# Both layers' first two output blocks as a Strassen pair, with both output pairs' P1 and P2 in front, in a two-layer trunk kernel on one core

## The chip, the cores and the metric

The kernel runs on one core of a Trainium2 chip. The metric is the device time of one execution in microseconds (us). A core has a matrix engine (TensorE, PE in the profile; its weight loads are listed apart as PEld), a vector engine (VectorE, DVE), a scalar engine (ScalarE, ACT), a general engine (GpSimd, POOL) and a synchronising engine (SyncE, SP), each with an instruction stream of its own that it works off in order. Here SP issues the loads from device memory, and POOL most of the writes. TensorE adds up its results in PSUM; the kernel uses eight banks of 128 x 512 float32.

## The reference

Two layers of a streaming encoder over 512 tokens of width 2048. One input projection per layer, then a group of four gated-linear-attention (GLA) heads and a group of eight chunked-attention heads, then one output projection with a norm and the residual:

```python
def hybrid_layer(x, w_in, w_out, g_pre, g_post, w_alpha, b_alpha, g_gla, g_att, rel_bias):
    h = rmsnorm(x, g_pre)
    z = h @ w_in
    gq, gk, gv, gg, ga, aq, ak, av, ag = split_columns(z)
    ...
    o_gla = rmsnorm(o_gla, g_gla...) * jax.nn.silu(gg)
    o_att = rmsnorm(o_att, g_att...) * jax.nn.silu(ag)
    y = jnp.concatenate([o_gla, o_att], axis=-1) @ w_out
    return x + rmsnorm(y, g_post)
```

The GLA state runs over chunks of 64 tokens, `S_c = a_c * S_(c-1) + k_c^T v_c`, so the second half of the tokens needs the state at the end of the first.

## The kernel before

**Jobs.** All projections are cut into blocks of 512 output columns: fourteen of the input, then four of the output, W0 to W3 (`NB_IN` to `NB_IN + 3`). The unit of the stream of weights is a *job* (`class Job`, L174): 256 rows by 512 columns of weights (512 KB). SP loads it (`raw`, for a Strassen product also `H`), VectorE forms a sum or difference of two blocks where a product needs one (L240, L243), ScalarE writes the rounded high part `wh` (L251), VectorE the rest as low part `wl` (L257, three buffers in turn, L255). TensorE multiplies high by high, high by low and low by high, so that the result is near to float32. `prepare` and `ahead` (L285, L299) keep loads and parts a few jobs in front of TensorE.

**Two ways to multiply.** A block on its own (`std_gemm`, L360; matmuls L380) takes eight jobs of 24 matmuls. Two blocks together can be done as a Strassen pair (`class Pair`, L406; matmuls L504, or L491 with features on the partitions): seven products P1 to P7 over four chunks each, 28 jobs of 12 matmuls, where two single blocks take 16 jobs of 24. P1, P2 and P4 use the operands as they are (P4 with a combined weight); P5, P6, P3 and P7 use the sums S1 to S4 of quarters of the left operand. P1+P2 is token half 0 of the first block, P7, P3 and P4 close the other three. A pair has two pairs of PSUM banks, X and Y: P1 goes to X, P5 to Y, P6 to X, and so on (`target`, L414). `seeded` means that P2 goes on in the banks of P1, and that these are seeded again from a copy of P1 later (`open`, L435).

**Stages of a layer.** Three input pairs whose P1 and P2 stand in front of everything (`HEAD`), two pairs for queries and keys, one for the GLA keys and queries, one for the GLA values (GV0, GV1; order P1, P5, P6 and P3 mixed, P7, P2, P4 by `PROD`, L145). Then the output projection: W0 for all tokens, W1 for token tiles 0 and 1, the pair W2 and W3 (`W23`, order P1, P2, P5, P6 and P3 mixed, P7, P4 by `PROD_END`, L152), W1 again for token tiles 2 and 3 with its weights read a second time.

**Around the output projection.** The GLA heads are worked in units of one head and one token half (`class Unit`, L1238; `gla_heads`, L1336), both halves of two heads in a row once their value block is there. `output_sums` (L804, through `make_sums`, L753) loads the finished heads from memory (`t<-fa`, `t<-fg`), forms S1 to S4 of the output pair on VectorE (L765), splits each into high and low (L113, L114) in slots g0 to g3, and writes them out (`oS<-g`, POOL); SP loads them again as left operands (`sa<-oS`, L230). `project` (L1426) takes a closed PSUM bank out: ScalarE squares it for the norm (L1433), VectorE multiplies it by the gain (L1436). The gain is loaded by `load_gain` (L1420) into a tile from `t2()` (L77), a pool of eight buffers used in turn, which the four parts of every chunk of the sums and the squares use too. `finish` (L1463) ends with `finish_token` (L1447): norm, residual, and the write of a token tile (128 tokens) to memory. Work beside the matmuls (heads, sums, finishing) stands in a list of tasks that is worked off at a rate per job; the order on each engine comes from a scheduler over the recorded program.

## Time and profile before

| | |
|---|---|
| time, median of 3 runs | 1603.68 us (1603.67 to 1607.72) |
| profiled execution | 1604.27 us |
| its span, first to last instruction | 1601.9 us |
| TensorE's mean granted clock | 0.998 |
| loaded from and written to memory | 393.01 MB, 72.11 MB |

A row of a group of instructions reads: line, engine, operation, what it writes and reads, shape, number | busy us, mean ns of one | idle time of the engine just before them and what ended most of it. Names are those of the program without their numbers, and a number behind "x" is a count. A matmul's mean is longer than the distance between two of them, since they overlap. In the windows each engine has its busy us with the number of instructions, and behind them the granted clock (1.00 is full), the share of the sixteen DMA engines and GB/s.

### The profile page before, as it was taken

The numbers are of one execution on the slowest core, as the hardware profiler recorded it, in microseconds if no ns is written. First come the engines' busy times: TensorE is split into PE (matmuls) and PEld (weight loads), VectorE is DVE, ScalarE is ACT, GpSimd is POOL, SyncE is SP. The second block draws the span as 40 slices with busy tenths as digits, with TensorE's granted clock in tenths as the row PEclk, the third lists the DMA queues.
The fourth block names the chain that finished last, engine by engine and source line by source line (L and its number), as shares of the span: only waits on it lengthen the run. The fifth ranks groups of instructions, "written<-read, shape, count | busy, mean of one in ns | idle before, by whom it ended". The sixth has DMA issues, their size and how long they took to land.

```text
span 1601.9 us, 24514 instructions
## 1 busy us (share of the span) xinstructions
PE 1588.1 (99%) x8818; PEld 1353.9 (85%) x8818; DVE 1258.1 (79%) x1580; ACT 924.1 (58%) x1534; POOL 189.1 (12%) x302
## 2 busy tenths in 40 slices
PE   9999999999999999999999999999999999999997
PEld 6787889999988887788887888899999888777886
DVE  6888887786877876778868989768778778866886
ACT  8565544456676544555685556445666765355543
POOL 1131000001101101310312100000000011013110
PEclk9999999999999999999999999999999999999999
DMA  9999966858868698799868899668588677979995
GB/s 373 358 337 347 337 220 247 306 188 288 296 216 282 219 345 302 274 376 335 346 241 333 305 345 334 228 228 306 187 312 281 223 263 248 352 241 351 367 330 214
DMA packets 150616, 467.82 MB, mean 292 GB/s; under 512 B 16492, under 2 KB 35956, under 8 KB 150496
## 3 DMA queue, kind: packets, MB, share of 16 engines
q1 hardware_dynamic: 127232, 385.79, 67.7%
q0 software_dynamic: 22688, 79.53, 13.0%
q8 instruction: 69, 1.13, 0.3%
q10 hardware_dynamic: 576, 0.95, 0.2%
q14 instruction: 51, 0.42, 0.1%
HBM read 393.01 MB, written 72.11 MB: 290 GB/s over the span
## 4 chain that ended last, share of the span: by engine, by line
PE 92%; issue 3%; DMA 2%; DVE 1%; POOL 1%; ACT 1%; SPq 0%; POOLq 0%; DVEq 0%
PE mm L504 49%; PE mm L491 20%; PE mm L380 11%; PE ax L1089 2%; PE ax L504 1%; PE ax L1072 1%; PE ax L1255 1%; PE ax L1289 1%; DMA raw<-in_w_dram 1%; DMA H<-in_w_dram 1%; PE ax L1051 1%; PE ax L1052 1%; PE ax L1050 1%; PE ax L687 0%; DVE wl L257 0%
## 5 line engine op out<-in xcount | busy, mean ns | idle before, releaser
L251 ACT CAST wh<-raw 128x1024 fp32r<-128x1024 f32 x256 | 269.3, 1053 | 234.0 <-PE mm L504 97.3
L257 DVE TENSOR_TENSOR wl<-raw,wh 128x1024 fp32r<-128x1024 f32 x256 | 312.5, 1221 | 114.9 <-PE mm L504 36.2
L251 ACT CAST wh<-H 128x1024 fp32r<-128x1024 f32 x239 | 251.1, 1053 | 211.7 <-PE mm L504 88.7
L257 DVE TENSOR_TENSOR wl<-H,wh 128x1024 fp32r<-128x1024 f32 (+1 forms) x241 | 292.9, 1217 | 91.1 <-PE mm L504 36.5
L504 PE MATMUL mm<-wh,sa 128*128 128x512 f32 x1088 | 345.2, 392 | 0.1
L504 PE MATMUL mm<-wh,g 128*128 128x512 f32 x832 | 258.1, 389 | 0.0
L504 PEld LDWEIGHTS mm<-wh,sa 128*128 128x128 f32 x1088 | 203.2, 188 | 43.3 <-issue 1.5
L491 PE MATMUL mm<-sa,wh 128*128 128x256 f32 x1280 | 235.9, 285 | 0.0
L504 PE MATMUL mm<-wh,a 128*128 128x512 f32 x704 | 228.8, 396 | 2.2 <-ACT a L113 0.9
L504 PE MATMUL mm<-wl,sa 128*128 128x512 f32 x544 | 212.6, 391 | 0.0
L240 DVE TENSOR_TENSOR H<-H,raw 128x1024 f32<-128x1024 f32 x160 | 194.3, 1220 | 17.5 <-DMA raw<-in_w_dram 9.4
L491 PEld LDWEIGHTS mm<-sa,wh 128*128 128x128 f32 x1280 | 199.4, 192 | 0.3
L504 PEld LDWEIGHTS mm<-wh,g 128*128 128x128 f32 x832 | 156.2, 188 | 32.3
L491 PE MATMUL mm<-sa,wl 128*128 128x256 f32 x640 | 181.0, 283 | 0.0
L504 PE MATMUL mm<-wl,g 128*128 128x512 f32 x416 | 162.3, 390 | 1.1 <-DVE wl L257 1.1
L504 PEld LDWEIGHTS mm<-wh,a 128*128 128x128 f32 x704 | 131.6, 188 | 35.4 <-issue 4.9
L504 PE MATMUL mm<-wl,a 128*128 128x512 f32 x352 | 137.9, 393 | 0.6 <-DVE wl L257 0.5
L491 PEld LDWEIGHTS mm<-sa,wl 128*128 128x128 f32 x640 | 122.3, 191 | 0.1
L504 PEld LDWEIGHTS mm<-wl,sa 128*128 128x128 f32 x544 | 102.2, 188 | 21.3 <-DVE wl L257 0.3
L552 POOL TENSOR_TENSOR sm<-sm,cst 128x4 f32<-128x4 f32 (+2 forms) x40 | 59.4, 1486 | 321.6 <-DVE sm L1449 128.0
L491 PE MATMUL mm<-a,wh 128*128 128x256 f32 x512 | 94.4, 285 | 0.0
L504 PEld LDWEIGHTS mm<-wl,g 128*128 128x128 f32 x416 | 78.1, 188 | 18.9 <-DVE wl L257 2.6
(208 smaller groups left out, 2272.0 us busy)
## 6 DMA issues: line engine op xcount, KB each, us to landing
raw<-in_w_dram SPq DMA_DIRECT2D x352, 512.0 KB, 5.5
sa<-S SPq DMA_DIRECT2D x128, 512.0 KB, 4.7
H<-in_w_dram SPq DMA_DIRECT2D x63, 512.0 KB, 5.6
S<-g POOLq DMA_DIRECT2D x32, 512.0 KB, 6.4
g<-S SPq DMA_DIRECT2D x32, 512.0 KB, 5.2
sa<-A SPq DMA_DIRECT2D x32, 512.0 KB, 6.1
oS<-g POOLq DMA_DIRECT2D x32, 512.0 KB, 5.8
sa<-oS SPq DMA_DIRECT2D x32, 512.0 KB, 5.0
```

Of the source, the lines that this page charges most:

```text
L240: nc.vector.tensor_tensor(out=h, in0=h, in1=r, op=ALU.add)
L251: last_cast[0] = nc.scalar.copy(self.wh, src).ins
L257: last_low[0] = nc.vector.tensor_tensor(out=self.wl[:, kk, :], in0=self.src[:, kk, :], in1=self.wh[:, kk, :].bitcast(F32), op=ALU.subtract ...
L380: mm = nc.tensor.matmul(pss[o], a[:, part, t], rhs[:, kk, :], start=(i == 0 and kk == 0 and m == 0), stop=(i == n - 1 and kk == 1 and m == 2),
L491: nc.tensor.matmul(dst, lhs[:, kk, f], a[:, part, tok], start=(fresh and kk == 0 and m == 0 and ft % 2 == 0), stop=(c == self.last and kk ...
L504: nc.tensor.matmul(out_ps[t], a[:, part, tok], rhs[:, kk, :], start=(fresh and kk == 0 and m == 0), stop=(c == self.last and kk == 1 and m ...
L552: return nc.gpsimd.tensor_tensor(out=out_r, in0=v, in1=mhalf[:, : v.shape[-1]], op=ALU.pow).ins
L1050: nc.tensor.matmul(ps[:, :n], self.qh[:, t], self.kh[:, :n], start=True, stop=False)
L1051: nc.tensor.matmul(ps[:, :n], self.qh[:, t], self.kl[:, :n], start=False, stop=False)
L1052: nc.tensor.matmul(ps[:, :n], self.ql[:, t], self.kh[:, :n], start=False, stop=True)
L1072: nc.tensor.transpose(ps[:, j * P : (j + 1) * P], self.prob[i][:, j * P : (j + 1) * P], ident)
L1089: nc.tensor.matmul(o, self.pt[i][:, j * P : (j + 1) * P], av[hd // 4, j // 2][:, j % 2, (hd % 4) * P : (hd % 4 + 1) * P], start=(j == 0), ...
```

## The change

W0 and W1 become a Strassen pair as W2 and W3 are, in both layers (`PAIRED`). The stream of the output projection is now: W23's P1, W01's P1, W23's P2, W01's P2 (four jobs each), then the rest of W01 (P5, P6 and P3, P7, P4), then the rest of W23, 56 jobs of 12 matmuls. `paired_out` drives it and takes the place of the two `std_gemm` calls, of `w_consume` and of the second reading of W1. The value pair becomes an early, seeded pair: P1, P2, then the rest. The GLA units are started by token half: as soon as token half 0 of a value block is there, its two heads' first halves run, and `ends` keeps their last states for the second halves. The output sums are staged in g6, g7, g14 and g15. In the last layer the last three jobs of P4 are done bank by bank (`by_bank`), so that token tile 2 is taken out while tile 3 is multiplied. The core of the diff:

```diff
+    W01 = (NB_IN, NB_IN + 1)
     W23 = (NB_IN + 2, NB_IN + 3)
+    OUT = (W01[0], W23[0])
+    PAIRED = (0, 1)
...
         for b0, b1 in PAIRS:
-            pr = {"early": False}
-            stream += [Job(l, k, c, b0, b1, pr) for k, c in PROD]
+            pr = {"early": b0 == GV0}
+            order = early_head(C_IN) + early_rest(C_IN) if pr["early"] else PROD
+            stream += [Job(l, k, c, b0, b1, pr) for k, c in order]
+        if l in PAIRED:
+            outs = [(W01, {"early": True}), (W23, {"early": True, "second": True})]
+            for k, i in (("P1", 1), ("P1", 0), ("P2", 1), ("P2", 0)):
+                stream += [Job(l, k, c, *outs[i][0], outs[i][1]) for c in C_END]
+            for bs, pr in outs:
+                stream += [Job(l, k, c, *bs, pr) for k, c in early_rest(C_END)]
+            continue
...
+        def by_bank(self, prods, evac):
+            jobs = [take(self.l, self.b0, k, c) for k, c in prods]
+            closing = None
+            for t in range(2):
+                for job, (k, c) in zip(jobs, prods):
+                    with tc.issue_after(closing) if closing else nullcontext():
+                        self.matmuls(job, k, c, only=t)
+                closing = self.closing
+                evac(t, self.acc[self.target[k]][t])
...
-        return make_sums(l, True, ("g0", "g1", "g2", "g3"), parts, chunks)
+        return make_sums(l, True, ("g6", "g7", "g14", "g15") if l in PAIRED else ("g0", "g1", "g2", "g3"), parts, chunks)
...
-                for half in range(2):
+                for half in range(1 if paired else 2):
...
+        og, issued = {}, {"outer": 0, "states": 0}
+        ends = slot("g3", [4, 256])
...
+                if p == 0:
+                    self.st[3] = ends[:, h, :]
+                self.prev = ends[:, h, :] if p else None
...
-            yield from output_sums(l, (2,3,))
+            while not paired and issued["states"] < 8:
+                yield
+            yield from output_sums(l, (2, 3))
+            if paired:
+                while len(og) < 8:
+                    yield
+                yield from output_sums(l, (0, 1))
...
-        GV = {1: ("g4", "g5"), 0: ("g0", "g1")}
+        GV = {(0, 0): "g2", (1, 0): "g4", (1, 1): "g5", (0, 1): "g0"}
...
-            if h and t:
-                heads = gla_heads(j, [gv[j, p] for p in range(2)])
-                tasks.append(heads if j else beside(heads, early_sums(), 3))
+            if t:
+                heads = gla_heads([(2 * j, h), (2 * j + 1, h)])
+                tasks.append(beside(heads, early_sums(), 3) if (j, h) == (0, 1) else heads)
...
         def finish(pair, xs):
-            p4 = next(i for i, z in enumerate(stream) if z.l == l and z.b0 == W23[0] and z.kind == "P4")
-            while done["low"] < p4 + 4:
+            at, n = (("P4", 2) if last else ("P7", 2)) if paired else ("P4", 4)
+            first = next(i for i, z in enumerate(stream) if z.l == l and z.b0 == W23[0] and z.kind == at)
+            while done["low"] < first + n:
                 yield
...
+        def paired_out():
+            gains, held = {}, {}
+
+            def consume(n):
+                def f(j, h, t, src, comb):
+                    until(lambda: issued["states"] == 8)
+                    project(2 * h + t, n + j, settled(src, comb), gains[n + j])
+                    if (n + j, h, t) == (3, 0, 1):
+                        for i in range(8):
+                            del A[i // 4, 0, i % 4]
+                        tasks.append(finish(0, held["xs", 0]))
+                return f
+
+            def side(n):
+                def f(k, c):
+                    if (k, c) in (("P2", C_END[2]), ("P4", C_END[0])):
+                        gains[n] = load_gain(n)
+                    elif (k, c) == ("P6", C_END[2]):
+                        gains[n + 1] = load_gain(n + 1)
...
+                return f
+
...
+            ways = dict(early=True, end=True, scaled=False, seeded=True)
+            pairs = [
+                Pair(l, W01, consume(0), x_bank=flip, **ways),
+                Pair(l, W23, consume(2), x_bank=flip ^ 2, keep=early_kept, **ways),
+            ]
+            for k, i in (("P1", 1), ("P1", 0), ("P2", 1), ("P2", 0)):
+                pairs[i].run(products(C_END, k), rate=3, after=side(2 * i))
+            pairs[0].open(flip)
+            pairs[0].run(early_rest(C_END), rate=1.5, after=side(0))
+            pairs[1].open(flip ^ 2)
+            rest = early_rest(C_END)
+            pairs[1].run(rest[: -3 if last else None], rate=1.5, after=side(2))
+            if last:
+                def evac(t, ps):
+                    steps = finish_token(2 + t, held["xs", 1][t])
+                    project(2 + t, 2, ps, gains[2], lambda: next(steps))
+                    for _ in steps:
+                        pass
+
+                pairs[1].by_bank(rest[-3:], evac)
+            drain()
...
+            if not last:
+                tasks.append(finish(1, held["xs", 1]))
```

**How the order moves.** Three places are shown. The lines of the changed kernel are higher: L257 is L260 there, L504 is L517, L765 is L789, L1436 is L1478, L1457 is L1499.

TensorE, layer 0, where the first job of P5 begins. Before, W23's P1 and P2 stand in front of it; P2 is in the auxiliary banks `ax`, and P5 goes to `mm_7404`, the banks in which W1's token tiles 0 and 1 (`mm_7012`) had been added up eight jobs earlier:

```order
L504 MATMUL ax_7307<-wh_7298,a_1353_6826 128x512
L504 MATMUL ax_7307<-wl_7320,a_1353_6826 128x512
L504 MATMUL ax_7307<-wh_7298,a_1353_6826 128x512
L504 MATMUL mm_7404<-wh_7323,sa_7327 128x512
L504 MATMUL mm_7404<-wl_7341,sa_7327 128x512
```

In the changed kernel the last job of W01's P2 (into `mm_6705` and `mm_6706`) stands in front of W01's P5, whose banks `mm_7101` are those of W23's P1 and P2 (`mm_6555`, `mm_6556`), closed four jobs earlier:

```order
L517 MATMUL mm_6706<-wh_6989,a_1184_6072 128x512
L517 MATMUL mm_6706<-wl_7017,a_1184_6072 128x512
L517 MATMUL mm_6706<-wh_6989,a_1184_6072 128x512
L517 MATMUL mm_7101<-wh_7020,sa_7024 128x512
L517 MATMUL mm_7101<-wl_7038,sa_7024 128x512
```

What moved: four jobs of matmuls stand between the close of the earlier banks and their reuse, where eight stood.

VectorE, layer 0, around `project` of these banks. Before, W1's token tile 0 (`mm_7012`) is taken out between the low parts of W23's P1 jobs and the sums of the last chunks:

```order
L257 TENSOR_TENSOR wl_7156<-H_7107,wh_7130 128x1024
L114 TENSOR_TENSOR g_1415_7116<-t_1400_7033,g_1415_7116 128x512
L257 TENSOR_TENSOR wl_7201<-H_7132,wh_7158 128x1024
L765 TENSOR_TENSOR t_1423_7143<-t_1422_7142,t_1423_7143 128x512
L765 TENSOR_TENSOR t_1422_7142<-t_1420_7140,t_1422_7142 128x512
L1436 TENSOR_TENSOR g_1369_6944<-mm_7012,t_1393_7010 128x512
L257 TENSOR_TENSOR wl_7203<-H_7160,wh_7199 128x1024
```

In the changed kernel the list from the low part of the third job of P5 (`wl_7082`, whose buffer was last that of `wl_7017`, the last job of W01's P2) on is:

```order
L260 TENSOR_TENSOR wl_7082<-H_6591,wh_7062 128x1024
L243 TENSOR_TENSOR H_6522<-H_6522,raw_7087 128x1024
L789 TENSOR_TENSOR t_1378_6866<-t_1377_6865,t_1378_6866 128x512
L789 TENSOR_TENSOR t_1377_6865<-t_1375_6863,t_1377_6865 128x512
L114 TENSOR_TENSOR g_1382_6890<-t_1378_6866,g_1382_6890 128x512
L789 TENSOR_TENSOR t_1378_6866<-t_1378_6866,t_1375_6863 128x512
L114 TENSOR_TENSOR g_1383_6895<-t_1377_6865,g_1383_6895 128x512
L789 TENSOR_TENSOR t_1376_6864<-t_1376_6864,t_1378_6866 128x512
L243 TENSOR_TENSOR H_6573<-H_6573,raw_7140 128x1024
L114 TENSOR_TENSOR g_1384_6900<-t_1378_6866,g_1384_6900 128x512
L789 TENSOR_TENSOR t_1392_6930<-t_1391_6929,t_1392_6930 128x512
L789 TENSOR_TENSOR t_1391_6929<-t_1389_6927,t_1391_6929 128x512
```

and it goes on with:

```order
L114 TENSOR_TENSOR g_1388_6923<-t_1376_6864,g_1388_6923 128x512
L243 TENSOR_TENSOR H_6591<-H_6591,raw_7179 128x1024
L1478 TENSOR_TENSOR g_1405_6995<-mm_6555,t_1397_6958 128x512
L114 TENSOR_TENSOR g_1393_6936<-t_1392_6930,g_1393_6936 128x512
L1478 TENSOR_TENSOR g_1408_7001<-mm_6556,t_1397_6958 128x512
```

What moved: `project` of the reused banks (with the gain `t_1397`, which takes over the buffer of `t_1375`) now stands behind `wl_7082` and the 13 instructions that follow it: three sums of weights (L243) and ten instructions of the output sums. The sum whose low part is `g_1393` is the left operand of the fourth P5 job.

VectorE's last rows in layer 1. Before:

```order
L1449 TENSOR_REDUCE sm_15822<-ssy_14807 128x1
L1436 TENSOR_TENSOR g_2982_14809<-mm_15684,t_3179_15681 128x512
L1457 SCALAR_TENSOR_TENSOR bias_14825<-g_2982_14809,sm_15823,bias_14825 128x512
L1457 SCALAR_TENSOR_TENSOR bias_14826<-g_2982_14809,sm_15823,bias_14826 128x512
L1457 SCALAR_TENSOR_TENSOR sg_14827<-g_3153_15571,sm_15823,sg_14827 128x512
L1457 SCALAR_TENSOR_TENSOR sg_14828<-g_3153_15571,sm_15823,sg_14828 128x256 x2
```

Now:

```order
L1478 TENSOR_TENSOR g_3240_15767<-mm_15420,t_3245_15791 128x512
L1491 TENSOR_REDUCE sm_15859<-ssy_14837 128x1
L1499 SCALAR_TENSOR_TENSOR bias_15336<-g_3138_15303,sm_15845,bias_15336 128x512
L1499 SCALAR_TENSOR_TENSOR bias_15337<-g_3138_15303,sm_15845,bias_15337 128x512
L1499 SCALAR_TENSOR_TENSOR sg_15338<-g_3240_15767,sm_15845,sg_15338 128x512
L1499 SCALAR_TENSOR_TENSOR sg_15339<-g_3240_15767,sm_15845,sg_15339 128x256 x2
L1499 SCALAR_TENSOR_TENSOR g_3120_15226<-g_3056_14933,sm_15860,g_3120_15226 128x1024
L1499 SCALAR_TENSOR_TENSOR g_3121_15227<-g_3035_14839,sm_15860,g_3121_15227 128x1024
```

What moved: two 1024-wide pieces of token tile 1 now stand behind the last pieces of tile 3; tiles 0 and 1 are written through POOL's queue, tiles 2 and 3 through SP's and ACT's.

More of the change, by code (lines that the diff above doesn't have):

```diff
@@ L215, in bring @@
             k, c, p = self.kind, self.c, self.pair
-            end = self.b0 == W23[0]
+            end = self.b0 in OUT
             name = LEFT.get(k)
@@ L422, in __init__ @@
             self.first, *_, self.last = C_END if end else C_IN
+            self.by_tile = [(k, self.last) for k in ("P7", "P4", "P1")] + [(k, self.first) for k in ("P4", "P2")]
             self.acc, self.keep, self.kept = {}, {}, keep
@@ L475, in operand, with matmuls @@
             return S_on[self.l, LEFT[k], c]
-        def matmuls(self, job, k, c):
+        def matmuls(self, job, k, c, only=None):
             a = self.operand(job, k, c)
@@ L499, in matmuls @@
                     order.sort(key=lambda z: z[1])
+                if only is not None:
+                    order = [z for z in order if z[1] == only]
                 for kk, t in order:
@@ L518, in run @@
                     last_evac[0] = seeds[0]
-                ahead(held=int(k == "P7" and c == prods[prods.index((k, self.last)) - 1][1] and self.seeded))
+                ahead(held=int(self.seeded and (k, c) == ("P7", (C_END if self.end else C_IN)[2])))
                 if c == self.last:
@@ L857, in layer @@
         last = l == L - 1
+        paired = l in PAIRED
+        flip = 2 * (sum(z < l for z in PAIRED) % 2)
         if l:
@@ L1334, in turn, with gla_heads @@
                 og[p, h] = op
-        def gla_heads(j, gv):
+                if not A:
+                    return
+                if ("O", 0) in A:
+                    A[1, p, h] = op
+        def gla_heads(specs):
             units = []
             def new(k):
-                h, p = 2 * j + k // 2, k % 2
-                units.append(Unit(h, p, gv, units[-1] if p else None))
+                h, p = specs[k]
+                units.append(Unit(h, p, [gv[h // 2, z] if (h // 2, z) in gv else None for z in range(2)]))
                 units[-1].outer()
@@ L1349, in gla_heads @@
             yield
-            for k in range(4):
-                if k < 3:
+            for k in range(len(specs)):
+                more = k < len(specs) - 1
+                if more:
                     new(k + 1)
@@ L1385, in fetch_operands @@
                         nc.sync.dma_start(flat(op_att[0, i]), src)
-            if k == "P4":
+            if k == "P4" and not paired:
                 i = OO[c] - 4
@@ L1474, in layer @@
         x_src = x if l == 0 else x_mid
+        def paired_out():
[15 more added lines that the diff above has]
+                        gains[n + 1] = load_gain(n + 1)
+                    if n == 0 and k in ("P7", "P4") and c == C_END[0]:
+                        until(lambda: all((l, True, z, i) in made for z in ("S1", "S2", "S3", "S4") for i in range(4)))
+                        held["xs", int(k == "P4")] = load_tokens(int(k == "P4"), x_src, nc.gpsimd)
+                return f
+            until(lambda: all((0, i) in op_att or fetch_operands("end", 0) for i in range(4)))
+            for c in range(4):
+                A[0, 0, c] = op_att[0, c]
+            A["O", 0] = True
+            for (p, h), z in og.items():
+                A[1, p, h] = z
+            ways = dict(early=True, end=True, scaled=False, seeded=True)
[18 more added lines that the diff above has]
+            drain()
+            for c in range(4):
+                del A[1, 1, c]
+            del A["O", 0]
+            if not last:
+                tasks.append(finish(1, held["xs", 1]))
```

63 lines of the change are left out of this document (34 added, 29 removed).

## Prediction

> **What bounds the kernel now.** I read the page's busy times first, then the chain of work that ended last, then TensorE's waits.
>
> ```profile
> PE 1588.1 (99%) x8818; PEld 1353.9 (85%) x8818; DVE 1258.1 (79%) x1580; ACT 924.1 (58%) x1534; POOL 189.1 (12%) x302
> PE 92%; issue 3%; DMA 2%; DVE 1%; POOL 1%; ACT 1%; SPq 0%; POOLq 0%; DVEq 0%
> PE mm L504 <- DVE wl L257: 1.6, 4, 0.5
> PE mm L504 <- ACT pc L432: 0.8, 1, 0.8
> ```
>
> TensorE is busy for 99% of the span, 92% of the last chain is its own work, and the waits for other engines that the view lists come to a few microseconds in all. So the time is the number of matmuls, and a change gains what it takes off that number and loses every wait that it opens. VectorE at 79% is the next engine, an average that hides stages in which it is the tighter one. The price of a matmul comes from an undisturbed piece of the chain in the second half of layer 0's output projection:
>
> ```profile
> 725.00 52.13 PE mm L504 x230
> ```
>
> 52.13 / 230 = 0.2267 us each; a job of 12 takes 2.72 us. Every matmul in question is 128x512.
>
> **What goes.** W0 and W1 take per layer 8 x 24 + 8 x 12 + 8 x 12 = 384 matmuls before, and 28 x 12 = 336 as a pair: 48 fewer per layer, 96 in all, **-21.8 us**. No other count of TensorE changes. This is all that the change can bring, since TensorE hardly waits now.
>
> **What VectorE gets.** In number little: 32 sums of weights (H) more, the value pair's 8 P2 sums fewer, 8 low parts more, 16 half-wide ones fewer. What counts is where they stand.
>
> ```profile
> L257 DVE TENSOR_TENSOR wl<-raw,wh 128x1024 fp32r<-128x1024 f32 x256 | 312.5, 1221 | 114.9 <-PE mm L504 36.2 <-PE mm L491 22.3 <-ACT wh L251 17.2
> L240 DVE TENSOR_TENSOR H<-H,raw 128x1024 f32<-128x1024 f32 x160 | 194.3, 1220 | 17.5 <-DMA raw<-in_w_dram 9.4 <-DMA H<-in_w_dram 5.1 <-issue 1.8
> L114 DVE TENSOR_TENSOR g<-t,g 128x512 fp32r<-128x512 f32 x52 | 35.1, 687 | 7.7 <-ACT g L113 7.6
> L765 DVE TENSOR_TENSOR t<-t,t 128x512 f32<-128x512 f32 x32 | 22.1, 691 | 12.1 <-DMA t<-fg 11.8
> L1436 DVE TENSOR_TENSOR g<-mm,t 128x512 f32<-128x512 f32 x16 | 11.0, 687 | 5.2 <-ACT t L1433 5.2
> ...
> 697.41 1.29 DVE L114 TENSOR_TENSOR g<-t,g 128x512 fp32r<-128x512 f32 x2
> 698.62 1.22 DVE L257 TENSOR_TENSOR wl<-raw,wh 128x1024 fp32r<-128x1024 f32 x1
> 699.75 1.22 DVE L257 TENSOR_TENSOR wl<-H,wh 128x1024 fp32r<-128x1024 f32 x1
> ```
>
> Neighbours overlap a little: from start to start a wide one (1024) takes 699.75 - 698.62 = 1.13 us, two narrow ones (512) 698.62 - 697.41 = 1.21, so 0.605 each. All the narrow kinds above last alike (687 to 691 ns).
>
> **The new wait, at W01's P5.** P5 starts in the banks of W23's P1 and P2, and its first matmul has to wait until `project` has taken `mm_6555` out. In VectorE's order that `project` stands behind `wl_7082`. `wl` has three buffers, so `wl_7082`, the low part of P5's third job, can't be written before TensorE has finished the last job of W01's P2. Between that job and P5 TensorE has nothing else to do. From `wl_7082` to `project` the rows are four wide and eleven narrow: 4 x 1.13 + 11 x 0.605 = **11.2 us** per layer, with every operand at hand. That is the least that the wait can be, and it doesn't depend on how far VectorE is behind. Nothing hides it: ScalarE's casts and SP's loads run on, TensorE stands.
>
> Two other things say when `project` runs. I count from the start of W01's first P2 job; P5 is then due after 4 x 2.72 = 10.9 us. First, VectorE's list. The low part of W01's fourth P2 job can't be written until the first is done (three buffers), so it ends at 2.72 + 1.13 = 3.9. From there to `project` I count 10 wide and 19 narrow, 11.3 + 11.5 = 22.8: done at 26.7, a wait of 15.8. Second, the gain. `t_1397` takes over the buffer of `t_1375`, whose last reader is the fifth row behind `wl_7082`; up to there the list has 8 wide and 12 narrow, 3.9 + 9.0 + 7.3 = 20.2. SP can issue the gain's load only then.
>
> ```profile
> t<-in_g_post_dram SPq DMA_DIRECT2D x10, 256.0 KB, 6.8
> oS<-g POOLq DMA_DIRECT2D x32, 512.0 KB, 5.8
> sa<-oS SPq DMA_DIRECT2D x32, 512.0 KB, 5.0
> t<-fg SPq DMA_DIRECT2D x16, 256.0 KB, 6.3
> out_dram<-g POOLq DMA_DIRECT2D x4, 512.0 KB, 4.5
> out_dram<-sg SPq DMA_DIRECT2D x1, 256.0 KB, 2.6
> ...
> DMA to landing us min/median/max: 3.4/5.6/12.1
> ```
>
> The gain lands at 20.2 + 6.8 = 27.0, `project` ends 0.7 later, at 27.7: **a wait of 16.8 us per layer**. I take this one, since it is the last of the three by the medians. From above: a 256 KB load of the same stage (`t<-fg`, the last row) once took 12.1, which would add 5.3. Behind the gain in SP's queue stand two more gains, the operands of P5's third and fourth job and the next weights; they wait too, but TensorE waits already.
>
> A second wait follows. The fourth job's operand is the sum whose low part stands just behind `project`: 0.6 for it, 0.5 to issue, 5.8 to write, 5.0 to read it back, 11.9 us after P5's start, when three jobs have taken 8.2: **3.7 us** per layer, between nothing (were the loads quick) and 8. Before, the same reuse had eight jobs in between, 21.8 us, and this `project` stood ahead of the sums; its stage shows TensorE without a gap:
>
> ```profile
> core 0: us, PE busy (x) PEld busy (x) DVE busy (x) ACT busy (x) POOL busy (x), PEclk, DMA share, GB/s
> 0.00:4.00 4.00, 2.81 (x7) 1.04 (x8) 0.33 (x2) 1.35 (x2) 1.27 (x11) 1.00 0.57 163
> 669.90:703.70 33.80, 33.80 (x152) 27.96 (x152) 21.87 (x26) 17.84 (x29) 6.29 (x12) 1.00 1.02 392
> 703.70:725.50 21.80, 21.80 (x97) 18.04 (x97) 18.14 (x21) 10.79 (x16) 2.13 (x4) 1.00 0.94 357
> 725.50:779.60 54.10, 54.10 (x240) 44.80 (x239) 48.80 (x50) 29.03 (x39) 8.91 (x6) 1.00 0.93 351
> ...
> L827 PE MATMUL ax<-t 128*128 128x512 bf16 x10 | 4.4, 632 | 1.2 <-DVE t L824 1.2
> ```
>
> Layer 1 has the same order, so both waits count twice: 2 x (16.8 + 3.7) = +41.0.
>
> **Restarts.** No wait of this length is in the trace, but its start is one: the ten matmuls of L827, after nothing, took 4.4 us where ten at 0.2267 take 2.3, though the window shows a granted clock of 1.00. I take 2.1 us for each long wait, +4.3; the bounds are 0 (they are another kind, bf16) and four times 2.1.
>
> The Trainium skill, "TensorE: Matmul & The Clock Gate", section "What's actually happening", puts a price on this: an idle window of about 3.4 us drops the clock to half, and it is full again after about 3.4 us of work. By it, as an estimate, a restart loses 1.7 us, and the second wait, 3.7 us long, would cost one as well: four restarts, 6.8 us instead of 4.3, 1634.5 in all. The ten slow matmuls agree with the rule, the granted clock of 1.00 beside them doesn't show it.
>
> **The end.** VectorE's last rows are now two wide pieces of token tile 1, behind those of tile 3, and POOL's queue writes them.
>
> ```profile
> 1590.99 2.48 DVE L1457 SCALAR_TENSOR_TENSOR g<-g,sm,g 128x1024 f32<-128x1024 f32 x2 [0.15 <-POOL sm L552]
> ```
>
> Two pieces are +2.48, and a POOL write lands in 4.5 where SP's took 2.6: **+4.4 us**, at least 2.4 if the write lands as quickly.
>
> **Costed at nothing.** The value pair's new order and the GLA units by token half: the same matmuls and units, started earlier; their matmuls are the same in number, and VectorE's and ScalarE's part lies beside the value pair's own jobs. Without that cover a unit's chain would be waited for once, some microseconds. The seeds (six pairs of copies more on ScalarE) stand in front of a product of other banks; one copy that TensorE waited for cost 0.8 (the `pc` row), so 6 x 0.9 = 5.4 at most. SP's 34 more issues: 16 weights, 32 operands `sa<-oS` and 2 gains more, 16 operands fewer, 17 MB. In the rest of W23 they are densest: 36 loads of 0.52 MB in 20 jobs, 18.9 MB in 54.4 us, 347 GB/s; the windows show 351 to 392 with TensorE never waiting. Off POOL's queue go 8 writes.
>
> **The sum.** -21.8 + 41.0 + 4.3 + 4.4 = +27.9. The profiled execution took 1604.27 us (span 1601.9; 2.4 lie around it), the median of the runs is 1603.68: the two are within 0.6. 1604.3 + 27.9 = **1632 us**.
>
> **The rivals.**
>
> *The wait stays at its floor.* If VectorE had nothing left of its list by the end of P2 and the gain were there, the wait would be 11.2 a layer, the second one hidden and the restart free: -21.8 + 22.4 + 2.4 = +3.0, **1607**. For it: SP's loads are often quicker than the median (3.4 is the least of `t<-fg`). Against it: the gain's buffer comes free only by the fifth row behind `wl_7082`, which is inside the floor, and the list is 15.8 long.
>
> *The wait is absorbed; the kernel is not slower.* If the wait per layer is under (21.8 - 4.4) / 2 = 8.7 us with nothing behind it, the change breaks even; if it were all hidden, the time would be 1604.3 - 21.8 + 4.4 = **1587**. Place: the same P5. For it: before, eight jobs covered it. Against it: four do now, and the 11.2 behind `wl_7082` would have to be wrong, as by two narrow operations at a time.
>
> *The rest of W23 is bound by loads.* With the two token tiles written there, 2.1 MB, 21.0 MB have to move in 54.4 us, 386 GB/s; at the 351 of the window they take 59.8, +5.4 a layer: **1643** on top of the forecast. For it: the share is at 0.93 already. Against it: 392 stands in the window before at no cost.
>
> *The change doesn't do what it says* can hardly be: the order has 96 matmuls fewer.
>
> **How the numbers follow.** Forecast 0.78 (1632; with the first wait by the list, 15.8, and the second wait, the restarts and the end at their bounds 1617 to 1645), floor 0.10 (1607), absorbed 0.04 (1587), bound by loads 0.08 (1643). The range leaves out the absorbed case below; its low end is the floor, 1607. Above, the forecast with both gains as late as 12.1 (+10.6) and the seeds at their bound (+5.4) comes to 1648; I take 1649. About 0.3%, 4.8 us, is what a measurement can tell from no change: faster 0.04, the same 0.10 (the floor lies inside by a little), slower 0.86.
>
> **What would show it.** In the trace after: in each layer one gap of TensorE of 11 to 22 us in front of W01's first P5 job, put down to VectorE's `project` (L1478); VectorE busy through that gap; a load of a gain that lands late in it; a shorter gap three jobs later that ends with `sa<-oS`; matmuls slower for some microseconds after each; the last write going through POOL. It is wrong if the gap is under 9 us, if TensorE has more gaps elsewhere (value pair, rest of W23), or if the jobs in front of P5 are themselves held up.

## The result and the profile after

The changed kernel takes **1655.75 us** (median of 4 runs, 1651.79 to 1657.57), the kernel before 1604.56 beside it (4 runs, 1603.67 to 1607.72): a ratio of **1.0312, 95% interval 1.0288 to 1.0336**. The prediction's direction holds; 1632 and its range up to 1649 do not. The profiled execution took 1657.57 us, the longest of the four, with a span of 1655.8, +53.9 against the span before, and a mean granted clock of 0.981 (0.998 before).

The page's busy times and its chain of work that ended last, and then TensorE's longest waits (us in total, times, longest):

```profile
PE 1585.7 (96%) x8722; PEld 1340.5 (81%) x8722; DVE 1295.4 (78%) x1600; ACT 949.8 (57%) x1562; POOL 180.6 (11%) x294
PE 81%; DMA 9%; issue 4%; DVE 3%; ACT 2%; POOL 1%; SPq 0%; DVEq 0%; POOLq 0%; ACTq 0%
```

```profile
PE mm L517 <- DVE g L1478: 25.0, 1, 25.0
PE mm L517 <- issue: 23.3, 1, 23.3
...
PE mm L517 <- DMA sa<-oS: 0.7, 1, 0.7
```

TensorE has 96 matmuls fewer, but is busy for only 2.4 us less: what is left of it has become slower. Two waits, one in each layer, make 48.3 us, and 9% of the last chain is now DMA transfers, which were 2%. The forecast's second wait, for `sa<-oS` at P5's fourth job, is missing: that job starts without a gap at 722.03, and the 0.7 of the last row stand later, in front of 730.84.

The windows around the two waits, layer 0 and layer 1 (columns as in the windows of before):

```profile
640.00:687.00 47.00, 47.00 (x218) 35.31 (x217) 31.51 (x46) 25.75 (x48) 11.65 (x20) 1.00 0.76 266
687.00:711.00 24.00, 0.70 (x4) 0.30 (x3) 20.23 (x25) 11.06 (x20) 3.72 (x7) 0.55 1.04 411
711.00:732.00 21.00, 20.34 (x77) 16.21 (x78) 13.46 (x16) 9.75 (x12) 3.18 (x6) 0.86 0.97 362
...
1506.00:1531.50 25.50, 0.46 (x3) 0.22 (x2) 21.56 (x27) 11.65 (x20) 4.13 (x8) 0.55 1.04 407
```

While TensorE stands, VectorE is busy for 20.2 of 24 us, and the sixteen DMA engines are full: share 1.04 at 411 GB/s. The granted clock falls to 0.55 and shows 0.86 afterwards. TensorE's timeline, first P5 job of layer 0, shows what that means for single matmuls (start, duration; a start-to-start distance counts, not the duration):

```profile
710.76 0.76 PE L517 MATMUL mm<-wh,sa 128*128 128x512 f32 x1 [23.30 <-issue]
...
717.32 0.39 PE L517 MATMUL mm<-wl,sa 128*128 128x512 f32 x1
717.55 0.61 PE L517 MATMUL mm<-wh,sa 128*128 128x512 f32 x2
```

From 710.76 to 717.32 start 16 matmuls; at 0.2267 they would take 3.6 us, so 2.9 are lost. Counted in the same way layer 1 loses 2.3.

VectorE's timeline in layer 0, from the low part of W01's fourth P2 job to `project`, and the chain that released P5 in layer 1:

```profile
679.17 1.22 DVE L260 TENSOR_TENSOR wl<-raw,wh 128x1024 fp32r<-128x1024 f32 x1 [0.90 <-issue]
683.11 1.42 DVE L789 TENSOR_TENSOR t<-t,t 128x512 f32<-128x512 f32 x2 [2.72 <-DMA t<-fg]
...
702.73 0.69 DVE L114 TENSOR_TENSOR g<-t,g 128x512 fp32r<-128x512 f32 x1 [0.24 <-ACT g L113]
...
705.40 0.69 DVE L114 TENSOR_TENSOR g<-t,g 128x512 fp32r<-128x512 f32 x1 [0.65 <-ACT g L113]
...
709.97 0.69 DVE L1478 TENSOR_TENSOR g<-mm,t 128x512 f32<-128x512 f32 x1 [2.74 <-DMA t<-in_g_post_dram]
710.58 0.68 DVE L114 TENSOR_TENSOR g<-t,g 128x512 fp32r<-128x512 f32 x1
```

```profile
1490.99 12.40 DMA t<-fg
...
1520.55 9.95 DMA t<-in_g_post_dram
...
1531.31 3.75 PE mm L517 x8
```

The order of the rows is the forecast's: low part, sums of chunk 3 (`t<-fg`), gain, `project`, P5. The holes between them are new: VectorE itself waits for a part that took 12.4 us to land and for a gain that took 9.95.

The end: the last pieces of token tile 1 stand last and leave through POOL, as forecast. Behind the last matmul come 11.8 us (1644.0 to 1655.8) where 8.5 came before: +3.3.

```profile
1648.47 2.48 DVE L1499 SCALAR_TENSOR_TENSOR g<-g,sm,g 128x1024 f32<-128x1024 f32 x2
...
1651.24 0.53 POOL L1501 DMA_DIRECT2D out_dram<-g  x1 [0.63 <-DVE g L1499]
```

One item was in nobody's sum. The reads of the GLA states (`read`, matmuls with 64 output partitions) are the same 128 records, but cost more; the groups of TensorE's instructions, shapes apart, before and after, and then TensorE's timeline after:

```profile
L1289 PE MATMUL ax<-g,g 128*64 128x256 f32 x128 | 17.3, 392 | 0.0
```

```profile
L1320 PE MATMUL ax<-g,g 128*64 128x256 f32 x128 | 25.0, 394 | 0.0
```

```profile
656.62 1.08 PE L1320 MATMUL ax<-g,g 128*64 128x256 f32 x8
657.64 0.74 PE L517 MATMUL mm<-wh,a 128*128 128x512 f32 x2
...
659.47 0.65 PE L1320 MATMUL ax<-g,g 128*64 128x256 f32 x2
660.05 0.50 PE L517 MATMUL mm<-wh,a 128*128 128x512 f32 x1
```

The timeline shows why: a whole read of eight records takes 1.02 us from start to start, 0.26 for two; a lone pair of records between two projection matmuls takes 0.58, 0.32 more. Over both layers the reads stand in 28 pieces where 16 stood before, and 18 of them are such lone pairs.

### The profile page after: what moved, and what is told of

Read it like the earlier page. It is cut to its first block, busy times and chain, and to the rows that moved or that the text cites. A ratio compares the mean times of both kernels' runs of the same rounds, so it can differ in the third digit from the quotient of the medians.

```text
span 1655.8 us, 24428 instructions
## 1 busy us (share of the span) xinstructions
PE 1585.7 (96%) x8722; PEld 1340.5 (81%) x8722; DVE 1295.4 (78%) x1600; ACT 949.8 (57%) x1562; POOL 180.6 (11%) x294
## 3 DMA queue, kind: packets, MB, share of 16 engines
q0 software_dynamic: 21536, 75.33, 11.8%
## 4 chain that ended last, share of the span: by engine, by line
PE 81%; DMA 9%; issue 4%; DVE 3%; ACT 2%; POOL 1%; SPq 0%; DVEq 0%; POOLq 0%; ACTq 0%
PE mm L517 52%; PE mm L502 19%; DMA raw<-in_w_dram 3%; DMA H<-in_w_dram 2%; PE ax L1115 2%; DVE wl L260 1%; PE ax L1098 1%; PE ax L1320 1%; PE ax L1284 1%; DMA t<-fg 1%; DMA sa<-A 1%; PE ax L711 1%; DVE H L243 1%; PE ax L1078 1%; PE ax L1077 1%
## 5 line engine op out<-in xcount | busy, mean ns | idle before, releaser
L517 PE MATMUL mm<-wh,sa 128*128 128x512 f32 x1344 | 430.9, 396 | 50.7 <-DVE g L1478 25.0
L260 DVE TENSOR_TENSOR wl<-H,wh 128x1024 fp32r<-128x1024 f32 (+1 forms) x265 | 322.2, 1219 | 108.4 <-PE mm L517 51.4
L260 DVE TENSOR_TENSOR wl<-raw,wh 128x1024 fp32r<-128x1024 f32 x240 | 293.4, 1223 | 103.9 <-PE mm L517 44.1
L517 PEld LDWEIGHTS mm<-wh,sa 128*128 128x128 f32 x1344 | 253.4, 190 | 110.6 <-issue 54.1
L517 PE MATMUL mm<-wh,a 128*128 128x512 f32 x896 | 290.8, 398 | 2.3 <-ACT a L113 1.4
L517 PE MATMUL mm<-wh,g 128*128 128x512 f32 x896 | 278.5, 389 | 0.0
L517 PE MATMUL mm<-wl,sa 128*128 128x512 f32 x672 | 265.2, 395 | 0.6 <-DVE wl L260 0.6
L243 DVE TENSOR_TENSOR H<-H,raw 128x1024 f32<-128x1024 f32 x192 | 233.5, 1222 | 24.8 <-DMA raw<-in_w_dram 16.5
L517 PEld LDWEIGHTS mm<-wh,a 128*128 128x128 f32 x896 | 167.0, 188 | 47.1 <-issue 9.6
L517 PEld LDWEIGHTS mm<-wh,g 128*128 128x128 f32 x896 | 168.2, 188 | 34.7
L517 PE MATMUL mm<-wl,a 128*128 128x512 f32 x448 | 176.8, 396 | 2.0 <-DVE wl L260 1.9
L517 PE MATMUL mm<-wl,g 128*128 128x512 f32 x448 | 175.4, 392 | 1.5 <-DVE wl L260 1.5
L517 PEld LDWEIGHTS mm<-wl,sa 128*128 128x128 f32 x672 | 127.5, 190 | 28.8 <-issue 1.5
L517 PEld LDWEIGHTS mm<-wl,a 128*128 128x128 f32 x448 | 84.3, 188 | 22.4 <-DVE wl L260 4.2
L517 PEld LDWEIGHTS mm<-wl,g 128*128 128x128 f32 x448 | 84.1, 188 | 22.0 <-DVE wl L260 4.6
```

Source lines behind the costliest of these rows:

```text
L243: nc.vector.tensor_tensor(out=h, in0=h, in1=r, op=ALU.add)
L260: last_low[0] = nc.vector.tensor_tensor(out=self.wl[:, kk, :], in0=self.src[:, kk, :], in1=self.wh[:, kk, :].bitcast(F32), op=ALU.subtract ...
L517: mm = nc.tensor.matmul(out_ps[t], a[:, part, tok], rhs[:, kk, :], start=(fresh and kk == 0 and m == 0), stop=(c == self.last and kk == 1 ...
```

## The experiments

Each was run once, with the kernel before beside it (1603.7 to 1605.5 us). The four runs of the changed kernel lie 5.8 us apart, so a difference of a few us between two single runs says little by itself. What was open at first: whether the long wait hangs on the late gain, on the sums around `project`, or on the four jobs of cover, and whether the value half costs its time by its split reads. Letters of theories are those of the expectations.

**e1_gains.** The gains of the first taking-out get a slot of their own, so that they can be loaded early.

```diff
+        def load_gain(n, gp=None):
+            gp = t2() if gp is None else gp
...
+            first = slot("g13", [2, 512])
...
-                        gains[n] = load_gain(n)
+                        gains[n] = load_gain(n, first[:, n // 2, :] if k == "P2" else None)
```

> The gains of W23's and W01's first taking-out lie in a slot of their own (g13) and are loaded as soon as TensorE's order passes W23's P2, so that they are there in time; all else as changed. Theory A (the wait at W01's P5 is VectorE's list plus a late gain): the waits of 23.3 and 25.0 us lose the idle times of VectorE just ahead of project, 2.7 and 2.9, and become 20.6 and 22.1; the time falls by 5 to 6 us to about 1650. Theory B (the gain is the cause, the list would be done): the waits fall to about 11 to 12 each, the time to about 1630.

1658.84 us, no gain. TensorE's waits:

```profile
PE mm L517 <- DVE g L1478: 32.0, 2, 16.5
PE mm L517 <- DMA sa<-oS: 11.3, 5, 3.7
```

The first wait falls to 16.5 and 15.5, between the two theories, but five waits for operands behind it take the place of much of what went, and the time doesn't fall. So the late gain was real, but taking it away alone gains nothing: the sums behind it are as late.

**e2_first.** In addition, the sums of the last two chunks are recorded only when W23's token half 0 has been taken out.

```diff
-                while len(og) < 8:
+                while len(og) < 8 or "projected" not in issued:
...
+                    if t:
+                        issued["projected"] = 1
```

> As e1, and the sums of the last two chunks are handed to VectorE only behind project of W23's P1 and P2, so that project stands ahead of them in its order. Theory A (the place of project behind the sums makes the wait): the waits at P5's first job go below 2 us each, and the time falls by some 45 us plus the slow restarts, to 1605 to 1610. Theory C (the sums themselves are late, whatever stands in front): TensorE waits as long as before minus what the list in front of project took, but now for the operand of P5's third or fourth job; from the sums' place in the list, 22 rows or some 17.5 us, plus 0.6, 0.5, 6.5 to write and 4.5 to read, against 8.2 us of jobs, about 17 us a layer, the time 1640 to 1645.

1663.0 us. Its timeline, rows of VectorE and TensorE:

```profile
676.78 0.68 DVE L1478 TENSOR_TENSOR g<-mm,g 128x512 f32<-128x512 f32 x1
...
683.45 1.42 DVE L789 TENSOR_TENSOR t<-t,t 128x512 f32<-128x512 f32 x2 [3.48 <-DMA t<-fg]
...
690.19 0.50 PE L517 MATMUL mm<-wl,sa 128*128 128x512 f32 x1 [1.61 <-DVE wl L260]
707.55 0.77 PE L517 MATMUL mm<-wh,sa 128*128 128x512 f32 x1 [14.79 <-DMA sa<-oS]
```

`project` runs at 676.78, before P5 is due, and the forecast's wait is gone. One of 14.8 us stands at P5's *second* job instead, on S1 of chunk 3: the sum is late whatever `project` does. The theory of late sums holds, one job earlier than it had said; its time, 1640 to 1645, was missed by 18 us.

**e3_reads.** The value half by itself: the four reads of a unit are chained so that they stand together.

```diff
-                for tt in range(2):
-                    for cc in range(2):
+                mm = None
+                for tt in (1, 0):
+                    for cc in (1, 0):
...
+                        with tc.issue_after(mm) if mm else nullcontext():
+                          mm = nc.tensor.matmul(
```

> The four matmuls that read a unit's states are recorded with the last state first and the others behind it, so that they stand together on TensorE as they did in the kernel before; in the changed kernel five of the eight units of a layer have them apart. Theory A (each piece that stands alone between matmuls of the projection costs TensorE a change of shape, about 0.7 us): the busy time of the reads falls from 25.0 to about 17.3 us, the stretch of value pair and P1, P2 gets 5 us shorter in each layer, the time about 1645. Theory B (the reads are slower for another reason, as the operands' slots): their busy time stays at 25 and the time at about 1655.

1646.79 us, 9.0 below the changed kernel's median; the span (1645.0) is 10.8 shorter than that of its profiled execution, with the two long waits nearly as they were (22.6 and 22.5, 3.2 less together). The group of reads, now 8.1 us cheaper:

```profile
L1322 PE MATMUL ax<-g,g 128*64 128x256 f32 x128 | 16.9, 390 | 0.0
```

**e4_swap.** W23's P1 and P2 first, then W01's P1 and P2, so that `project` has eight jobs as cover, not four.

```diff
-            for k, i in (("P1", 1), ("P1", 0), ("P2", 1), ("P2", 0)):
+            for k, i in (("P1", 1), ("P2", 1), ("P1", 0), ("P2", 0)):
```

> P1 and P2 of W23 in front of P1 and P2 of W01, so that eight jobs (21.8 us) instead of four stand between the close of W23's P2 and W01's P5. In VectorE's order project of W23 then stands ahead of the sums, and project of W01's P1 and P2 stands behind them, four jobs of P5 ahead of its reuse by P6. Theory A (the distance of close and reuse decides): no wait at P5's first job; at P6's first the list behind the low part of P5's third job takes about as long as now, 20 to 25 us from the end of P2, less the 10.9 of P5: 10 to 14 us a layer, the time 1628 to 1636. Theory C (the sums are late): TensorE waits 15 to 20 us at P5's third or fourth job, the time 1640 to 1650.

1648.9 us. P5's first wait is 0.8; its second job again waits for S1 of chunk 3:

```profile
703.73 0.76 PE L517 MATMUL mm<-wh,sa 128*128 128x512 f32 x1 [13.82 <-DMA sa<-oS]
```

The forecast's mechanism (four jobs between a bank's close and its reuse) can thus be taken away for 7 us in all. Why the sums are late is seen in chunk 3's own rows. Its S1 is made from the second half of head 3, which POOL writes to memory (`fg<-t`), and POOL then writes S1 (`oS<-g`). The two writes and the first matmul on sums before, and the two writes in the changed kernel (timelines):

```profile
632.66 0.54 POOL L1332 DMA_DIRECT2D fg<-t  x1 [2.17 <-ACT t L1328]
...
660.93 0.53 POOL L773 DMA_DIRECT2D oS<-g  x1 [0.39 <-DVE g L114]
...
724.84 0.39 PE L504 MATMUL mm<-wh,sa 128*128 128x512 f32 x1
```

```profile
649.39 0.54 POOL L1363 DMA_DIRECT2D fg<-t  x1 [0.34 <-ACT t L1359]
...
685.48 0.54 POOL L797 DMA_DIRECT2D oS<-g  x1 [8.36 <-DVE g L114]
```

Before, S1 of chunk 3 is written 64 us ahead of P5's first matmul. In the changed kernel it is written 25 us later, and P5 is due at 687.5, 37 us earlier: 2 us after the write has been issued, and the read has still to follow. In e2 the parts of chunk 3 are loaded from 668.17 to 671.68, behind the sums of chunk 2, whose buffers they take over; the last part is there at 683.4, S1 is written from 685.81, its read stands behind other loads in SP's queue until 697.00, and the operand is there at 707.55. The last half-head (head 1, transposed until 675.4 in the changed kernel) belongs to chunk 1, P5's fourth job, and isn't part of this chain. The standard jobs of W0 and W1, which need no sums, had been the cover of the chain.

**e5_direct** keeps S1 of the last two chunks (0 and 1) in SBUF as operands of W01's P5 (not read back from memory for these), forms the two S1 first, and has e2's and e3's edits. **e6_direct_swap** is the same with e4's order.

```diff
+            if end and not p.get("second") and (self.l, name, c) in resident:
+                self.a = resident[self.l, name, c]
+                return
...
+            order=[(n, c) for n in ("S1", "S2", "S4", "S3") for c in chunks] if late else None,
+            stay={("S1", 0): "g9", ("S1", 1): "g10"} if late else {},
```

> e2 and e3 together, and the S1 of the last two chunks stays in two slots (g9, g10) as the left operand of P5's third and fourth job, instead of being written to memory and read back; the sums of these chunks run S1, S1, S2, S2, S4, S4, S3, S3. Theory C (the chain from the last GLA unit through memory and the sums to P5's third job is longer than the jobs that lie beside it): the round trip of some 11 us falls out, the waits of 14.8 and 13.3 us at P5's third job (e2) go to about 3 to 5, the reads give 5 us a layer, the slow restart goes with the long wait; the time is 1608 to 1620. Theory D (VectorE has too much to do in this stretch, whatever comes first): the wait only moves on to the low parts and to later operands, and the time stays above 1635.

> As e5, with P1 and P2 of W23 in front of those of W01 as in e4. Theory C: the same chain ends at the same place, so that the time is that of e5 within 4 us. If the close of W23's P2 so near to P5 still costs something in e5 (2 to 3 us a layer were left at P5's first job in e2), this is faster than e5 by 4 to 6 us.

1630.82 and 1630.01 us, between the times of e5's two theories: e5 is 16 below e3, and the order of the products makes no difference to the time any more, though in e6 the wait of layer 1 (10.1 us) is put down to ScalarE's copy of the seeds and not to an operand. The chain of e5 up to P5's second job:

```profile
662.93 11.62 DMA raw<-in_w_dram
...
686.68 9.70 DMA sa<-oS
696.38 0.14 issue
696.52 0.76 PE mm L521
```

S1 of chunk 3 still goes through memory and is waited for 11.7 us. On the way stand loads of 512 KB that take 9.7 to 11.6 us to land, where the medians before were 7.6 (`raw`) and 7.4 (`sa`) between 640 and 725.

**e7_values_only** starts from the changed kernel again, takes the output pairs back (`PAIRED = ()`) and leaves the value pair and the half-heads; **e12_values_reads** is e7 with e3's reads.

> Only the other half of the change: no layer has W0 and W1 as a pair (W0 and W1 as before, PAIRED empty), the value pair is early and the GLA units go by token halves. No matmul fewer than before. Theory A/C (the pair's P5 makes the wait, the split reads cost 5 us a layer): no wait above 3 us anywhere, the reads at about 25 us if they are apart here too, the time 1604 to 1616. Rival (the GLA units by token halves finish so late that any output stage waits): a wait of several us ahead of W0's last chunks or of W1, the time above 1620.

> e7 with the four reads of a unit together as in e3. Theory A (the split reads are what the value half costs): the reads' busy time falls from 22.0 to about 17.3 us, the time from 1618.6 to 1608 to 1613. Rival (the value half costs by its waits and not by the reads): 1616 or more.

1618.63 us (1605.50 beside it) and 1608.34 (1605.01): the half of the change that was costed at nothing costs 13.1 us, and 3.3 with the reads together. The 3.3 are about what TensorE waits longer there (8.4 us of waits in all, 5.2 before). No version with only this half gains anything.

**e8_chunk3** is e5 with chunk 3's S1 resident too, its parts in slots of their own instead of the turning buffers, and the first gains in the buffers of the copies. **e9_chunk3_tail** is e8 with `finish` of the last layer let go at P7, as in layer 0; **e10_rate** is e9 with the tasks beside P1 and P2 worked off twice as fast.

```diff
+            if c == 3 and l in PAIRED:
+                tiles = [z[:, k, :] for z in (slot("g2", [2, 512]), slot("g13", [2, 512])) for k in range(2)]
...
+            stay={("S1", 0): "g9", ("S1", 1): "g10"} if late else {("S1", 3): "g12"} if l in PAIRED else {},
...
-            at, n = (("P4", 2) if last else ("P7", 2)) if paired else ("P4", 4)
+            at, n = ("P7", 2) if paired else ("P4", 4)
...
-                pairs[i].run(products(C_END, k), rate=3, after=side(2 * i))
+                pairs[i].run(products(C_END, k), rate=6, after=side(2 * i))
```

> As e5; and the four parts of chunk 3 of the output sums come into two slots of their own (g2, g13) instead of the eight turning buffers, its S1 stays in a slot (g12) as the operand of P5's second job, and the first two gains lie in the buffers of the copies (ev). In e5 the wait of 11.7 us stood at P5's second job, whose operand is the S1 of chunk 3. Theory E (the eight turning buffers make it: chunk 3's parts can't be loaded before chunk 2's sums are done, and these stand in VectorE's list behind low parts that wait for TensorE): VectorE sums chunk 3 some 15 us earlier, the waits of 11.7 and 11.8 go below 3 in total each layer, and the time is 1600 to 1610. Theory C alone (the last GLA unit ends too late): the waits move to the third job and stay at 6 to 10 us, the time 1620 to 1630.

> As e8, and in the last layer the token tiles 0 and 1 are finished from P7 on and not from P4, so that VectorE's last rows are those of tile 3 as in the kernel before. Expected: 2 to 4 us faster than e8, the last transfer being one of 256 KB on SP's or ACT's queue. Rival (the end is set by tile 3 in both): the same time as e8 within 1 us.

> As e9, with six steps of the waiting tasks per job instead of three while P1 and P2 of the output pairs run, so that the last GLA units are recorded earlier. Theory C: what wait is left at P5's third job falls by up to one job (2.7 us) per layer, 2 to 5 us faster than e9. If the wait is gone in e9 already: the same time within 2 us.

1636.12, 1635.71 and 1638.11 us: none beats e5, and e8's forecasts (1600 to 1610, 1620 to 1630) both fail. e9 is 0.4 faster than e8 where 2 to 4 were expected, and e10 is 2.4 slower than e9. In e8 the wait of 11.7 is gone, but shorter ones stand around its place; TensorE's timeline of layer 0:

```profile
693.37 1.22 PE L521 MATMUL mm<-wh,g 128*128 128x512 f32 x2 [2.44 <-ACT g L113]
...
695.31 1.63 PE L521 MATMUL mm<-wh,g 128*128 128x512 f32 x3
...
728.59 0.76 PE L521 MATMUL mm<-wh,sa 128*128 128x512 f32 x1 [5.05 <-DMA sa<-oS]
...
729.57 1.05 PE L521 MATMUL mm<-wh,sa 128*128 128x512 f32 x2
```

Slow matmuls follow them, such as three in 1.44 us from 695.31 and, behind the last, two in 0.86 from 729.57. All waits of TensorE add up to 36.8 us in e8 and 40.2 in e5, and still e8 is 5.3 slower. By subtraction it loses in its rate what it saves in waiting (mean granted clock 0.987, in e5 0.990); with one run of each that isn't shown. In e9 the end behind the last matmul does fall, from 11.7 to 8.3 us, but the last matmul ends 3.1 later, so 0.4 is left.

**e11_operands_early** asks what the pair would give if no operand were late: on e9 without the resident S1, W01's P5, P6 and P3 take chunk 2's sums for every chunk, so that the output is no longer the layer's. **e13_fewer_loads** also reads each of these sums only once.

```diff
+            if self.b0 == W01[0] and k in ("P5", "P6", "P3"):
+                c = 2
```

> Part of the computation is changed: P5, P6 and P3 of W01 take the sums of chunk 2 for all four chunks, which are there long before; all sums are still formed, written and read, so that loads, VectorE and ScalarE have the same work. The rest is e9 without the slots for S1: chunk 3's parts and the first gains in places of their own, the reads together, the tail as before. Theory C (what is waited for is the chain from the last GLA units to the operands): no wait above 2.5 us in the output stage, the time near 1604 - 22 + 2 x 4 for the value stage, 1588 to 1596. Theory D (VectorE's list and SP's queue are too full here, whatever the operands): waits for low parts, H and raw of 6 us or more a layer stay, the time above 1605.

> e11 (W01's P5, P6 and P3 take the sums of chunk 2 for all chunks), and now each of the three is read from memory once per layer instead of four times: 9 loads of 0.52 MB, 4.7 MB, fewer per layer in a stretch where the DMA engines moved 412 GB/s without a break. VectorE's and ScalarE's work and all else as in e11. Theory F (what was left in e11 is the DMA engines' ceiling: 4.7 MB at 412 GB/s are 11.4 us): the waits left in the output stage of e11, some 10 us a layer, mostly go, and the slow restarts with them; the time falls by 16 to 28 us to 1602 to 1614. Theory D (VectorE's list): the time stays within 5 us of e11's 1630.

1630.42 and 1631.4 us: no better than e5. In e11 a stretch of loads takes the place of the late sums; two windows of its layer 0, and its loads from 670 to 740 (KB each, median us to landing):

```profile
700.00:720.00 20.00, 15.59 (x66) 11.69 (x65) 18.07 (x22) 11.87 (x17) 2.76 (x6) 1.00 1.03 416
720.00:740.00 20.00, 17.18 (x75) 13.56 (x74) 15.64 (x16) 7.66 (x11) 1.51 (x3) 1.00 1.03 410
```

```profile
raw<-in_w_dram SPq DMA_DIRECT2D x16, 512.0 KB, 11.2
sa<-oS SPq DMA_DIRECT2D x16, 512.0 KB, 10.8
```

TensorE is busy for 15.6 and 17.2 of 20 us with the DMA engines full. In e13 they are not (371 GB/s), TensorE is busy for 66 of 70 us, and the time stays. The window, and TensorE's timeline a little earlier:

```profile
670.00:740.00 70.00, 65.97 (x271) 51.08 (x269) 57.97 (x66) 35.34 (x55) 12.11 (x19) 0.95 0.97 371
```

```profile
621.52 0.94 PE L1362 MATMUL ax<-cst,bias 128*128 128x128 f32 x4 [1.63 <-DVE bias L1352]
...
624.01 1.06 PE L526 MATMUL mm<-wh,sa 128*128 128x512 f32 x2
624.87 0.63 PE L526 MATMUL mm<-wl,sa 128*128 128x512 f32 x1
```

So full DMA engines aren't the whole of it. What is left in e13 is many waits of up to 3 us, for low parts, casts and copies above all (32.4 us of waits in all, 5.2 before), with slow matmuls behind the one shown (three in 1.28 us, 0.43 each). Which of these would have to go for the 21.8 us to show was not separated; **that stays open**.

## Why the prediction was right in direction and wrong in size

| step | forecast | measured |
|---|---|---|
| 96 matmuls fewer | -21.8 | 96 records fewer; -21.8 at 0.2267 |
| first wait, both layers | +33.6 | +48.3 (23.3 and 25.0) |
| second wait | +7.4 | 0 at P5's fourth job, +0.7 later |
| slower matmuls behind the waits | +4.3 | +5.2 (2.9 and 2.3) |
| value pair and half-heads | 0 | +10.8 from the split reads (e3), +3.3 besides (e12) |
| the end | +4.4 | +3.3 |
| sum | +27.9 | +49.8 of the span's +53.9 |

The rows come from separate runs, so the sum is rough: in e3 the two long waits are also 3.2 us shorter, which the row of the first wait already has, and between e7 and e12 the same edit of the reads gave 9.8. All other waits of TensorE, each under 1 us but for the first of the program, add up to 9.1 us after and 5.2 before, which is about the 4.1 left over; no run was made for them.

*The first wait.* The step was right in place, order and count: the trace has the 10 wide and 19 narrow rows of the list, and they took 23.8 us where 22.8 were counted (680.39, the end of the low part, to 710.58, less 6.35 of idle time). What failed is **"with every operand at hand", and the gain's 6.8 us beside it**. VectorE idles for 2.72 + 0.24 + 0.65 + 2.74 = 6.35 us in this list. In layer 1 the gain alone accounts for it: by the chain it was issued at 1520.55, 25.2 behind the start of W01's P2 (the end of the idle time less its length and four jobs, 1495.4), where 20.2 were counted, and took 9.95 instead of 6.8, which makes 8.2 more than 16.8: 25.0. The durations came from medians over the whole run before, both layers. In the window of before that the forecast showed for this stage (669.9 to 703.7, 392 GB/s, share 1.02), the DMA view has three gains and four `t<-fg` (median us to landing last):

```profile
t<-fg SPq DMA_DIRECT2D x4, 256.0 KB, 12.1
t<-in_g_post_dram SPq DMA_DIRECT2D x3, 256.0 KB, 7.6
```

So most of the slow landing could have been read there. The row of 3.4 / 5.6 / 12.1 was used for the range (+5.3 a layer), but not for the forecast.

*The second wait* didn't come in the changed kernel, and not because of the longer first one: its sum stands just behind `project` and moves with it. The forecast set 11.9 us of low part, write and read against 8.2 us of three jobs. In layer 0 the three jobs took 11.3 (710.76 to 722.03), since their matmuls were slow, a term that the forecast had and didn't carry into this one; and between 709 and 724 a write and a read landed in 4.5 us each (medians), where 5.8 and 5.0 were taken. In e1 and e2, with the first wait shorter or gone, waits for these sums come in its place.

*The restarts* were sized about right. The Trainium skill's rule ("TensorE: Matmul & The Clock Gate", section "What's actually happening") gives 1.7 us by the forecast's estimate; 2.9 and 2.3 were measured. It puts the limit at an idle window of about 3.4 us; here waits of 1.63 and 2.44 us already have matmuls at half rate behind them (e13 at 621.52, e8 at 693.37), while one of 2.46 us has none (e13 at 1614.20), so the limit doesn't hold here as a sharp one.

*Costed at nothing* was the second error: **"the same matmuls and units, started earlier; their matmuls are the same in number"**. Equal numbers are not equal time, as e3 showed with an edit of order alone. The Trainium skill has a rule that was overlooked: "TensorEngine Tiling (Array Packing)", section "Key Properties", says that a change of tiling mode drains the engine. The 0.32 us more of a lone pair of reads agrees with that; no run separates a drain from other costs of the change of shape. e7 shows the same error from the other side: this half alone makes the kernel slower.

*SP's loads* were weighed as a rate over the rest of W23, with the verdict that 392 GB/s had been borne. They came together earlier, in the gap itself, at 411 GB/s, and cost landing times. That is the rival "bound by loads" in kind, but in another place, and not by itself: in e13 fewer loads left the time as it was.

*The rivals.* Floor and absorbed are out: the wait is twice 11.2. The deeper point is one that the forecast didn't have as a rival: it took the reuse of the banks for the cause. e2 and e4 take that reuse away, and in each layer a wait of 13 to 15 us stays, now put down to an operand.

*What would show it* named most of the signs (one gap per layer at P5 with VectorE busy, a late gain, slow matmuls, a write by POOL last). The gap of 11 to 22 us was 23.3 and 25.0, and the shorter gap three jobs later didn't come. Of the value pair only gaps were named as a sign of being wrong; the reads opened none there and cost their time as slower work.

The best version with both output pairs is e6, 1630.0 us, 25.7 below the changed kernel and 24.5 above the one before it ran beside. No version in this study beat the kernel before, and what keeps the pair's 21.8 us from showing is only shown in part.

## What to carry to other kernels

Before work is taken off the engine that bounds a kernel, look at what that work covers: here cheap standard jobs covered a chain of two trips through memory, and the chain came to light as soon as they went. A gap that is put down to a buffer's reuse should be checked for the next thing that would be late at the same place. Take landing times from the stage's own window and not from the whole run, and price an instruction by its neighbours as well as by its number.

## What was unexpected of the hardware

- Half-rate matmuls (0.43 us from start to start, not 0.2267) can follow waits as short as 1.63 us, and even a wait of 23 us loses only 2.9 us behind it. In these runs waits of 2.5 us or more were always followed by them, and of the waits from 1.6 to 2.5 us some were (1.63 in e13, 2.44 in e8) and some not (1.75 in e4 at 709.93, 2.46 in e13 at 1614.20).
- A lone pair of 64-partition reads between 128 x 512 matmuls takes 0.58 us, in a block of eight 0.26; grouping them gave 10.8 us of span (e3) and 9.8 of time (e7 to e12).
- Near 410 GB/s on one core the DMA engines are full (share 1.03 to 1.04), and a load of 512 KB landed after 10.8 to 11.2 us (e11, 670 to 740, median) instead of 7.4 to 7.6 (before, 640 to 725, mean 328 GB/s).
